# Hybrid decoder trunk on one core: six pairs of the first up projection's wide group as seven-product sets, with side work that pauses

## The chip, the cores and the metric

The kernel runs on one core of one Trainium2 chip. The metric is the device time of one execution in microseconds (us); the figure of a version is the median of its runs. The engines are TensorE (PE; its weight loads are shown as PEld), VectorE (DVE), ScalarE (ACT), GpSimd (POOL) and SyncE (SP). Each has a queue of its own and works through it in order. They wait for one another by semaphores. DMA transfers are issued here from SP (weights) and from POOL (side work).

## The reference

Two layers of a decoder over 256 positions of width 2048. What matters here, cut:

```python
for layer in range(DEPTH):
    if layer % 2 == 0:
        mix = even_mixer(h, ...)   # SSD heads and MoBA attention heads, then one output projection
    else:
        mix = odd_mixer(h, ...)    # NSA attention heads and retention heads, then one output projection
    h = layer_norm(DEEPNORM_ALPHA * h + mix, ...)
    ffn = conv_ffn(h, ffn_w_up[layer], ffn_conv_w[layer], ffn_conv_b[layer], ffn_w_down[layer])
    h = layer_norm(DEEPNORM_ALPHA * h + ffn, ...)

def conv_ffn(x, w_up, conv_w, conv_b, w_down):
    a, u = jnp.split(x @ w_up, 2, axis=-1)
    a = causal_depthwise_conv(a, conv_w, conv_b)
    return (jax.nn.silu(a) * u) @ w_down
```

`w_up` has 2 x 5632 columns. All is float32.

## The kernel before

**Products in three matmuls.** A float32 product is made of reduced-precision parts: each weight slab comes by DMA into one of six buffers `wraw` (L185), ACT copies its rounded value `whi` (L210), DVE subtracts to get the rest `wlo` (L218), and PE adds three products, high by high, high by low and low by high. `Weights.get` keeps the splits three slabs ahead of PE (`AHEAD = 3`); there are four buffers each for `whi` and `wlo`.

**Groups.** A projection runs as a list of jobs. `group_b` (matmuls on L427) makes 256 columns of the output over all 16 k tiles of x; a slab holds four k tiles. `group_m` (L539 to L541) makes 1024 columns and takes the k tiles in pairs. A pair is a two by two block product: k tiles by the two halves of 256 positions, against the two halves of 1024 columns. Planned "P" (plain) it is 8 products of three matmuls. Planned "N" or "R" it is a set of 7 products after the Strassen-Winograd scheme, which needs sums of weight blocks and sums of activation blocks. For "N" the weight sums are made on the spot by four DVE additions (`add_up`, L229), into the tile `other` in an up projection. For "R" they were made earlier: the slab "T" is loaded from a DRAM scratch. An "N" pair loads two slabs of 512 KB, an "R" pair three of 512 KB and one of 256 KB, a "P" pair two of 512 KB. The activation sums come from `sum_up` (L499 on; L509, L513 and the splits on L337 and L338).

**The up projections.** `ffn(layer)` runs `group_b` for most of the 44 column blocks; block 7 of layer 0, and blocks 4, 8 and 12 of layer 1, are "wide": one `group_m` with `inner` makes four groups' columns. In both layers its eight pairs are planned "NPNPNPNP".

**Work between the matmuls.** `Fill` is a list of steps; after every second k tile of a `group_b` one step is popped from `self.fill` and one from `self.aux`. A number in the list is that many empty steps. In `ffn`, `self.fill` carries the side work: `cycles` makes the weight sums for later sets ("R"), one set at a time in the tile `sums` (or two in turn with `second`). A set is two loads issued by POOL (L240), the additions on DVE (L246), two stores issued by POOL (L250). Its period in steps is the third figure of `CYCLES` per layer (13 and 14; 10 for the six sets of layer 0 that use two tiles). `self.aux` carries the residual's multiplications (L873, L877) and the `sum_up` calls. Inside a `group_m` with `inner` only `self.aux` is popped. The tile framework orders instructions on an engine by readiness, except those that are pinned with `keep_in_program_order`; loads, additions and stores of the side work are pinned.

**The first attention.** In `even`, twelve `group_b` jobs (four gates z, then queries and keys of eight heads) run with the SSD scan and the attention heads as steps in `self.fill` at rate 0.80; nothing is in `self.aux` there. The scan makes decay products on DVE (L1340) that PE uses (L1355); POOL adds squares (L1368) and takes a power (L1378) that PE uses in `scale` (L1387). An attention head ends in `mix` (L1161), which multiplies the probabilities by V.

Of the kernel before, what the change touches and what calls it, by code (L numbers as in the profile page):

```python
# [34 lines left out]
        ("od_in", 0): "NPNPNPNP", **{(f"up{i}", p): "NPNPNPNP" for i in range(2) for p in range(3)}}  # L35
WIDE_UP = ((7,), (4, 8, 12))
FIRST = (22, 30)
CYCLES = ((6, 10, 13), (0, 0, 14))
SEVEN = {"down0": (1, 3, 5, 7, 9, 11, 13, 15, 16, 17, 14), "down1": (1, 3, 5, 7, 9, 11, 13, 14, 15),
         "ev_out": (0, 1, 2, 3), "od_out": (0, 1, 2, 3),  # L40
         "od_in": (0, 1, 2, 3), "up0": (0, 1, 2, 3), "up1": (0, 1, 2, 3)}
# [81 lines left out]
class Weights:  # L123
# [107 lines left out]
    def make(self, key, dram, s):  # L231
# [12 lines left out]
        def add():  # L244
            for o, x, y in ((b11, b11, b12), (b12, b12, b22), (b22, b11, b22), (b21, b22, b21)):
                self.tc.keep_in_program_order(nc.vector.tensor_tensor(o, x, y, op=OP.add))  # L246
# [5 lines left out]
        return load, add, store  # L252
# [69 lines left out]
class Trunk:  # L322
# [160 lines left out]
    def cycles(self, keys, bufs, period):  # L483

        fill, made = self.fill, [self.w.make(k, self.dram, bufs[i % len(bufs)]) for i, k in enumerate(keys)]
        n, wait = len(bufs), min(5, period - 4)
        fill.add(made[0][0])
        if n == 1:
            fill.add(period - 4 - wait)
        else:  # L490
            fill.add(3, made[1][0], 6)
        for i, (_, add, store) in enumerate(made):
            fill.add(add, 1, store)
            if i + n < len(made):
                fill.add(wait, made[i + n][0])
            if i + 1 < len(made):
                fill.add(period - 4 - wait)

    def sum_up(self, act, pair, u):  # L499
# [10 lines left out]
        a11, a21, a12, a22 = v[:, 0, :128], v[:, 0, 128:], v[:, 1, :128], v[:, 1, 128:]  # L510
        s1, s2, s4, s3 = (u[:, 128 * i:128 * i + 128] for i in range(4, 8))
        for o, p, q in ((s1, a21, a22), (s2, a11, s1), (s4, a12, s2), (s3, a21, a11)):
            nc.vector.tensor_tensor(o, p, q, op=OP.subtract)  # L513
        self.split(hi, lo, u[:, 512:896])
        self.split(*last, s3)

    def group_m(self, act, src, p, c, gap=1, fresh=None, inner=None):
# [73 lines left out]
        it = iter(index)  # L591
        for j, plan in pairs:
            k = 2 * j
            if plan != "P":
# [3 lines left out]
                add("P2", at(k + 1, 0), wt, 0)  # L598
                add("P3", s4, wt, 512)
                wt = w.get(next(it))  # L600
                add("P4", at(k + 1, 1), wt, 0)
# [11 lines left out]
            else:  # L613
                for kk in range(k, k + 2):
                    wt = w.get(next(it))
                    for n, t, o in (("P2", 0, 0), ("P4", 1, 0), ("P3", 0, 512), ("B8", 1, 512)):
                        add(n, at(kk, t), wt, o, whole and kk == 2 * pairs[-1][0] + 1)
# [468 lines left out]
    def attn_steps(self, P, y, ct, h, branches, gate=None, cmp=None):  # L1086
# [61 lines left out]
        def mix():  # L1148
            o = self.ps()
            for t in range(2):  # L1150
                mms = []
                for b, (_, _, v) in enumerate(branches):
                    pt = st["pt"][b]
                    if t == 0:
                        mms.append((v(0), pt[:, 0:128]))
                    else:
                        mms += [(v(0), pt[:, 128:256]), (v(1), pt[:, 256:384])]
                if cmp:
                    mms.append((cmp[0], cmp[1][:, t * 128:(t + 1) * 128]))
                for i, (a, b) in enumerate(mms):  # L1160
                    nc.tensor.matmul(o[:, t * 128:(t + 1) * 128], a, b, start=(i == 0), stop=(i == len(mms) - 1))  # L1161
            self.split(y[:, ct, :256], y[:, ct, 256:], o[:, :256])
# [4 lines left out]
    def even(self):  # L1167
        nc, x = self.nc, self.x
        with ExitStack() as ctx:
# [63 lines left out]
            with self.tc.tile_pool(name="even2", bufs=1) as P2:  # L1233
# [5 lines left out]
                self.fill.rate = 0.80  # L1239
                for i in range(4):  # L1240
# [392 lines left out]
    def ffn(self, layer):  # L1633
        nc, x = self.nc, self.x
        with ExitStack() as ctx:
# [11 lines left out]
            if wide:  # L1647
# [66 lines left out]
            for i, e in enumerate(evacs[3:], 3):  # L1714
# [11 lines left out]
                elif j not in wide and j - 1 not in wide:  # L1726
# [142 lines left out]
```

## Time and profile before

| | |
|---|---|
| runs | 2248.83 us median of 3 (2248.74 to 2249.03) |
| profiled execution | span 2246.8 us from the first to the last instruction; its own time outside the span isn't recorded beside it |
| first attention phase (twelve `group_b`) | 133 to 297 us |
| `up0`, with its wide group | 372 to 820 us; wide group about 528 to 568 us |
| `up1`, first of its three wide groups | about 1611 to 1651 us |
| mean granted TensorE clock | 0.999 |

The phases' bounds are read from the chain of work in order of time and from the timeline. A row of a timeline reads: start, duration, engine, line, operation, tiles, shapes, count, and in brackets the idle time of the engine before it with what ended it. A row of the waits reads: who waited for whom, total us, times, longest. Durations of neighbouring matmuls overlap; the pace of PE is the distance of their starts.

### The profile page before, as it was taken

How to read it: one execution, taken by the hardware profiler on the slowest of the kernel's cores; microseconds unless marked ns; L12 is line 12 of the kernel's file. 1: busy time of each engine (PE TensorE's matmuls, PEld its weight loads, DVE VectorE, ACT ScalarE, POOL GpSimd, SP SyncE). 2: the span in 40 equal slices, each digit the busy share in tenths (PEclk: the TensorE clock that was granted, in tenths of full speed). 3: DMA queues.
4: the chain of work that ended last, by engine and by line, in shares of the span. 5: the costliest groups of instructions: out<-in, count | busy, mean ns of one | idle time of the engine just before them, and what ended most of it. 6: DMA issues, size and time to landing. Idle time of an engine off the chain costs nothing.

```text
span 2246.8 us, 32995 instructions
## 1 busy us (share of the span) xinstructions
PE 2235.3 (99%) x12125; PEld 1920.9 (85%) x12125; DVE 1831.3 (82%) x2795; ACT 1254.0 (56%) x1718; POOL 126.4 (6%) x219
## 2 busy tenths in 40 slices
PE   9999999999999999999999999999999999999998
PEld 9888888888888888888898888888888888888887
DVE  5788688988877778887977777889988887779887
ACT  5555555655555556656645564457555565557563
POOL 0101000110011100000000000000100001100000
PEclk9999999999999999999999999999999999999999
DMA  9854456897788886888668534467876768888884
GB/s 312 292 175 161 158 194 189 274 376 264 238 302 302 296 284 213 292 286 274 211 208 287 188 114 154 152 209 235 290 227 228 255 217 297 300 273 276 276 280 169
DMA packets 158780, 546.33 MB, mean 243 GB/s; under 512 B 17827, under 2 KB 19283, under 8 KB 158483
## 3 DMA queue, kind: packets, MB, share of 16 engines
q1 hardware_dynamic: 132937, 451.41, 60.1%
q0 software_dynamic: 25536, 92.55, 11.8%
q8 instruction: 95, 1.56, 0.3%
q14 instruction: 68, 0.56, 0.1%
q10 hardware_dynamic: 144, 0.26, 0.0%
HBM read 502.19 MB, written 41.96 MB: 242 GB/s over the span
## 4 chain that ended last, share of the span: by engine, by line
PE 96%; DVE 2%; issue 1%; ACT 0%; POOL 0%; DMA 0%; SPq 0%; ACTq 0%; POOLq 0%; DVEq 0%
PE acc L427 51%; PE ps L540 7%; PE ps L541 7%; PE ps L539 7%; PE acc L627 3%; PE acc L629 3%; PE acc L628 3%; PE acc L540 3%; PE acc L541 3%; PE acc L539 3%; PE ps L628 1%; PE ps L627 1%; PE ps L629 1%; PE ps L1161 1%; PE ps L427 1%
## 5 line engine op out<-in xcount | busy, mean ns | idle before, releaser
L210 ACT ACTIVATE whi<-wraw 128x1024 fp32r<-128x1024 f32 (+4 forms) x882 | 875.1, 1002 | 549.6 <-PE acc L427 219.0
L218 DVE TENSOR_TENSOR wlo<-wraw,whi 128x1024 fp32r<-128x1024 f32 (+4 forms) x882 | 1007.5, 1153 | 209.6 <-ACT whi L210 197.6
L427 PE MATMUL acc<-x,whi 128*128 128x512 f32 x3296 | 1032.2, 398 | 0.0
L427 PEld LDWEIGHTS acc<-x,wlo 128*128 128x128 f32 x3296 | 604.0, 188 | 136.5 <-DVE wlo L218 0.3
L427 PE MATMUL acc<-x,wlo 128*128 128x256 f32 x3296 | 633.8, 279 | 0.0
L427 PEld LDWEIGHTS acc<-x,whi 128*128 128x128 f32 x3296 | 510.0, 189 | 9.7 <-issue 1.1
L689 ACT ACTIVATE tmp<-acc 128x512 f32<-128x512 f32 x104 | 62.2, 598 | 167.8 <-PE acc L427 167.7
L246 DVE TENSOR_TENSOR sums<-sums 128x512 f32<-128x512 f32 x140 | 96.2, 687 | 10.5 <-DMA sums<-in_down 9.4
L540 PE MATMUL ps<-wlo,g 128*128 128x512 f32 x260 | 101.3, 390 | 0.0
L541 PE MATMUL ps<-whi,g 128*128 128x512 f32 x260 | 101.2, 389 | 0.0
L539 PE MATMUL ps<-whi,g 128*128 128x512 f32 x260 | 101.2, 389 | 0.0
L539 PE MATMUL ps<-whi,x 128*128 128x512 f32 x244 | 94.0, 390 | 2.7 <-ACT whi L210 2.7
L540 PE MATMUL ps<-wlo,x 128*128 128x512 f32 x244 | 95.5, 391 | 0.1
L541 PE MATMUL ps<-whi,x 128*128 128x512 f32 x244 | 95.0, 389 | 0.0
L627 PE MATMUL acc<-whi,x 128*128 128x344 f32 (+3 forms) x224 | 74.9, 336 | 0.7 <-ACT whi L210 0.7
L628 PE MATMUL acc<-wlo,x 128*128 128x344 f32 (+3 forms) x224 | 74.5, 333 | 0.3 <-DVE wlo L218 0.3
L629 PE MATMUL acc<-whi,x 128*128 128x344 f32 (+3 forms) x224 | 74.3, 332 | 0.0
L1681 DVE SCALAR_TENSOR_TENSOR c<-fpad,prm,c 128x256 f32<-128x256 f32 x176 | 74.2, 479 | 0.0
L210 ACT ACTIVATE whi<-other 128x1024 fp32r<-128x1024 f32 x32 | 33.7, 1055 | 57.7 <-DVE other L229 56.9
L250 POOL DMA_DIRECT2D sumdown<-sums x62 | 33.3, 537 | 570.9 <-DVE sums L246 570.8
L540 PEld LDWEIGHTS ps<-wlo,g 128*128 128x128 f32 x260 | 48.8, 188 | 10.5 <-DVE wlo L218 0.4
L539 PEld LDWEIGHTS ps<-whi,g 128*128 128x128 f32 x260 | 48.8, 188 | 10.3
(458 smaller groups left out, 3141.6 us busy)
## 6 DMA issues: line engine op xcount, KB each, us to landing
wraw<-in_up SPq DMA_DIRECT2D x328, 512.0 KB, 4.8
wraw<-in_down SPq DMA_DIRECT2D x142, 512.0 KB, 4.8
wraw<-in_od_in SPq DMA_DIRECT2D x96, 512.0 KB, 4.2
wraw<-in_ev_in SPq DMA_DIRECT2D x72, 512.0 KB, 4.1
wraw<-sumdown SPq DMA_DIRECT2D x68, 512.0 KB, 4.5
sums<-in_down POOLq DMA_DIRECT2D x62, 512.0 KB, 6.8
sumdown<-sums POOLq DMA_DIRECT2D x62, 512.0 KB, 5.4
wraw<-in_ev_out SPq DMA_DIRECT2D x30, 512.0 KB, 3.9
```

Source lines behind the costliest of these rows:

```text
L210: a = nc.scalar.activation(hi[:, :n], raw[:, :n], AF.Copy)
L218: b = nc.vector.tensor_tensor(lo[:, :n], raw[:, :n], hi[:, :n].bitcast(F32), op=OP.subtract)
L246: self.tc.keep_in_program_order(nc.vector.tensor_tensor(o, x, y, op=OP.add))
L427: nc.tensor.matmul(acc, wt, mv, start=(k == 0 and i < len(unit)), stop=(k == nk - 1 and i >= len(unit)))
L539: nc.tensor.matmul(o, xh, wh, start=n not in used, stop=False)
L540: nc.tensor.matmul(o, xh, wl, start=False, stop=False)
L541: nc.tensor.matmul(o, xl, wh, start=False, stop=stop)
L627: nc.tensor.matmul(o, xh, wh, start=start, stop=False)
L628: nc.tensor.matmul(o, xh, wl, start=False, stop=False)
L629: nc.tensor.matmul(o, xl, wh, start=False, stop=stop)
L689: nc.scalar.activation(t, a[:, :, 256:], AF.Copy, scale=sign)
L1681: nc.vector.scalar_tensor_tensor(c[:, i, :], pad[:, i, t:t + 256], w[:, t:t + 1], c[:, i, :], op0=OP.mult, op1=OP.add)
```

## The change

- The plan of the wide group of `up0` goes from "NPNPNPNP" to "RRRPRRRP": six sets whose weight sums are loaded, two plain pairs. Six activation sums are made for it, in six tiles `part` instead of four.
- The six sets' weight sums are made in the first attention phase, by `cycles` with period 14 in `self.aux`.
- In `cycles` the additions of a set are separate steps, and they are three operations instead of four (one over 1024 columns makes two sums). The waits between steps are laid out anew; the period of layer 1 goes from 14 to 12.
- Eight empty steps are put at the head of `self.fill` before the last `group_b` ahead of each wide group.
- `sum_up` makes two of its four subtractions in one.
- `mix` multiplies by V(0) once over 256 positions instead of twice over 128.
- Stop flags in `group_m` follow the new order of the pairs.

```diff
-        ("od_in", 0): "NPNPNPNP", **{(f"up{i}", p): "NPNPNPNP" for i in range(2) for p in range(3)}}
+        ("od_in", 0): "NPNPNPNP", ("up0", 0): "RRRPRRRP", **{("up1", p): "NPNPNPNP" for p in range(3)}}
-CYCLES = ((6, 10, 13), (0, 0, 14))
+CYCLES = ((6, 10, 13), (0, 0, 12))
-         "od_in": (0, 1, 2, 3), "up0": (0, 1, 2, 3), "up1": (0, 1, 2, 3)}
+         "od_in": (0, 1, 2, 3), "up0": (0, 1, 2, 3, 4, 5), "up1": (0, 1, 2, 3)}
...
-        def add():
-            for o, x, y in ((b11, b11, b12), (b12, b12, b22), (b22, b11, b22), (b21, b22, b21)):
-                self.tc.keep_in_program_order(nc.vector.tensor_tensor(o, x, y, op=OP.add))
+        first, both = s[:, 0:1024].rearrange("p (i c) -> p i c", i=2), s.rearrange("p (i c) -> p i c", i=4)[:, 1:4:2, :]
+
+        def add(o, x, y):
+            return lambda: self.tc.keep_in_program_order(nc.vector.tensor_tensor(o, x, y, op=OP.add))
+
+        adds = [add(*a) for a in ((first, first, both), (b22, b11, b22), (b21, b22, b21))]
...
-    def cycles(self, keys, bufs, period):
+    def cycles(self, keys, bufs, period, fill=None):
...
-        n, wait = len(bufs), min(5, period - 4)
+        n = len(bufs)
         fill.add(made[0][0])
-        if n == 1:
-            fill.add(period - 4 - wait)
-        else:
+        if n == 2:
             fill.add(3, made[1][0], 6)
-        for i, (_, add, store) in enumerate(made):
-            fill.add(add, 1, store)
+        for i, (_, adds, store) in enumerate(made):
+            if n == 1:
+                fill.add(5)
+            fill.add(*adds, store)
+            if i + 1 < len(made):
+                fill.add(period - (10 if n == 1 else 6))
             if i + n < len(made):
-                fill.add(wait, made[i + n][0])
-            if i + 1 < len(made):
-                fill.add(period - 4 - wait)
+                fill.add(made[i + n][0])
+            if n == 2:
+                fill.add(1)
...
-        s1, s2, s4, s3 = (u[:, 128 * i:128 * i + 128] for i in range(4, 8))
-        for o, p, q in ((s1, a21, a22), (s2, a11, s1), (s4, a12, s2), (s3, a21, a11)):
+        s3, s1, s2, s4 = (u[:, 128 * i:128 * i + 128] for i in range(4, 8))
+        ends = u[:, 0:512].rearrange("p (i t) -> p i t", i=4)[:, 0:4:3, :]
+        for o, p, q in ((u[:, 512:768].rearrange("p (i t) -> p i t", i=2), a21[:, None, :].to_broadcast([128, 2, 128]), ends),
+                        (s2, a11, s1), (s4, a12, s2)):
             nc.vector.tensor_tensor(o, p, q, op=OP.subtract)
...
-                        add(n, at(kk, t), wt, o, whole and kk == 2 * pairs[-1][0] + 1)
+                        add(n, at(kk, t), wt, o, kk > k and (end or whole and n == "B8" and j == plain))
...
-            for t in range(2):
-                mms = []
-                for b, (_, _, v) in enumerate(branches):
-                    pt = st["pt"][b]
-                    if t == 0:
-                        mms.append((v(0), pt[:, 0:128]))
-                    else:
-                        mms += [(v(0), pt[:, 128:256]), (v(1), pt[:, 256:384])]
-                if cmp:
-                    mms.append((cmp[0], cmp[1][:, t * 128:(t + 1) * 128]))
-                for i, (a, b) in enumerate(mms):
-                    nc.tensor.matmul(o[:, t * 128:(t + 1) * 128], a, b, start=(i == 0), stop=(i == len(mms) - 1))
+            mms = [(v(0), pt[:, 0:256], 0) for (_, _, v), pt in zip(branches, st["pt"])]
+            mms[1:1] = [(v(1), pt[:, 256:384], 128) for (_, _, v), pt in zip(branches, st["pt"])]
+            if cmp:
+                mms[1:1] = [(cmp[0], cmp[1], 0)]
+            for i, (a, b, c) in enumerate(mms):
+                nc.tensor.matmul(o[:, c:256], a, b, start=(i == 0), stop=(i == len(mms) - 1))
...
                 self.fill.rate = 0.80
+                self.cycles(self.keys("up0"), [self.w.sums], 14, self.aux)
...
-                self.slots = [E.tile([128, 1024], F32R, name=f"part{i}") for i in range(4)]
+                self.slots = [E.tile([128, 1024], F32R, name=f"part{i}") for i in range(len(SEVEN[f"up{layer}"]))]
...
+                for step in sums[4:]:
+                    self.aux.add(3, step)
...
                 elif j not in wide and j - 1 not in wide:
+                    if j + 1 in wide and i % 2:
+                        self.fill.q[:0] = [lambda: None] * 8
                     self.group_b(x, [e])
```

More of the change, by code (lines that the diff above doesn't have):

```diff
@@ L250, in store @@
                 self.tc.keep_in_program_order(nc.gpsimd.dma_start(self.made[key][i], s[:, 1024 * i:1024 * i + 1024]))
-        return load, add, store
+        return load, adds, store
     def pump(self, n, pin=False):
@@ L481, in keys @@
         return [k for s in src for k in self.w.made if k[0] == s]
-    def cycles(self, keys, bufs, period):
-        fill, made = self.fill, [self.w.make(k, self.dram, bufs[i % len(bufs)]) for i, k in enumerate(keys)]
-        n, wait = len(bufs), min(5, period - 4)
+    def cycles(self, keys, bufs, period, fill=None):
+        fill, made = fill or self.fill, [self.w.make(k, self.dram, bufs[i % len(bufs)]) for i, k in enumerate(keys)]
+        n = len(bufs)
         fill.add(made[0][0])
-        if n == 1:
-            fill.add(period - 4 - wait)
-        else:
+        if n == 2:
             fill.add(3, made[1][0], 6)
-        for i, (_, add, store) in enumerate(made):
-            fill.add(add, 1, store)
+        for i, (_, adds, store) in enumerate(made):
[4 more added lines that the diff above has]
+                fill.add(period - (10 if n == 1 else 6))
             if i + n < len(made):
-                fill.add(wait, made[i + n][0])
-            if i + 1 < len(made):
-                fill.add(period - 4 - wait)
+                fill.add(made[i + n][0])
+            if n == 2:
+                fill.add(1)
     def sum_up(self, act, pair, u):
@@ L509, in sum_up @@
         nc.vector.tensor_tensor(v, act[:, k:k + 2, :256].bitcast(F32), act[:, k:k + 2, 256:].bitcast(F32), op=OP.add)
-        a11, a21, a12, a22 = v[:, 0, :128], v[:, 0, 128:], v[:, 1, :128], v[:, 1, 128:]
-        s1, s2, s4, s3 = (u[:, 128 * i:128 * i + 128] for i in range(4, 8))
-        for o, p, q in ((s1, a21, a22), (s2, a11, s1), (s4, a12, s2), (s3, a21, a11)):
+        a11, a21, a12 = v[:, 0, :128], v[:, 0, 128:], v[:, 1, :128]
+        s3, s1, s2, s4 = (u[:, 128 * i:128 * i + 128] for i in range(4, 8))
+        ends = u[:, 0:512].rearrange("p (i t) -> p i t", i=4)[:, 0:4:3, :]
+        for o, p, q in ((u[:, 512:768].rearrange("p (i t) -> p i t", i=2), a21[:, None, :].to_broadcast([128, 2, 128]), ends),
+                        (s2, a11, s1), (s4, a12, s2)):
             nc.vector.tensor_tensor(o, p, q, op=OP.subtract)
-        self.split(hi, lo, u[:, 512:896])
+        self.split(hi, lo, u[:, 640:1024])
         self.split(*last, s3)
@@ L591, in group_m @@
         it = iter(index)
+        plain = [j for j, plan in pairs if plan == "P"][-1]
         for j, plan in pairs:
             k = 2 * j
+            end = whole and j == pairs[-1][0]
             if plan != "P":
@@ L597, in group_m @@
                 wt = w.get(next(it))
-                add("P2", at(k + 1, 0), wt, 0)
-                add("P3", s4, wt, 512)
+                add("P2", at(k + 1, 0), wt, 0, end)
+                add("P3", s4, wt, 512, end)
                 wt = w.get(next(it))
-                add("P4", at(k + 1, 1), wt, 0)
+                add("P4", at(k + 1, 1), wt, 0, end)
                 fill.pop()
```

## The prediction

> **What bounds the kernel now.** I read the page first: the span, the engines' busy shares, and the chain that ended last.
>
> ```profile
> span 2246.8 us, 32995 instructions
> PE 2235.3 (99%) x12125; PEld 1920.9 (85%) x12125; DVE 1831.3 (82%) x2795; ACT 1254.0 (56%) x1718; POOL 126.4 (6%) x219
> ...
> PE 96%; DVE 2%; issue 1%; ACT 0%; POOL 0%; DMA 0%; SPq 0%; ACTq 0%; POOLq 0%; DVEq 0%
> ```
>
> TensorE (PE) is busy nearly all of the span and the chain is 96% PE. So only two things shorten the time: PE instructions that go, and PE waits that go. The next view is the list of PE's waits.
>
> ```profile
> PE ps L539 <- ACT whi L210: 2.7, 2, 1.5
> PE ps L1760 <- DVE ones L1757: 1.1, 1, 1.1
> ```
>
> The longest wait by far is at L539, inside `group_m`, twice in the whole run. The timeline places it: the second pair of the wide group of `up0` (539 us) and the second pair of the first wide group of `up1` (1622 us).
>
> ```profile
> 537.57 0.69 DVE L229 TENSOR_TENSOR other<-other,wraw 128x512 f32<-128x512 f32 x1
> 538.17 0.69 DVE L229 TENSOR_TENSOR other<-wraw 128x512 f32<-128x512 f32 x1
> 538.77 0.69 DVE L229 TENSOR_TENSOR other<-other,wraw 128x512 f32<-128x512 f32 x1
> 539.08 0.39 PE L539 MATMUL ps<-whi,part 128*128 128x512 f32 x1
> 539.58 1.06 ACT L210 ACTIVATE whi<-other 128x1024 fp32r<-128x1024 f32 x1 [6.08 <-DVE other L229]
> 540.69 0.50 PE L539 MATMUL ps<-whi,x 128*128 128x512 f32 x1 [1.22 <-ACT whi L210]
> 541.02 0.40 PE L540 MATMUL ps<-wlo,x 128*128 128x512 f32 x1
> ...
> 1615.02 0.69 DVE L246 TENSOR_TENSOR sums<-sums 128x512 f32<-128x512 f32 x1
> 1619.70 0.69 DVE L246 TENSOR_TENSOR sums<-sums 128x512 f32<-128x512 f32 x1
> 1621.50 0.69 DVE L229 TENSOR_TENSOR other<-other,wraw 128x512 f32<-128x512 f32 x1
> 1621.81 0.39 PE L539 MATMUL ps<-whi,part 128*128 128x512 f32 x1
> 1622.59 1.06 ACT L210 ACTIVATE whi<-other 128x1024 fp32r<-128x1024 f32 x1 [6.42 <-DVE other L229]
> 1623.69 0.50 PE L539 MATMUL ps<-whi,x 128*128 128x512 f32 x1 [1.50 <-ACT whi L210]
> ```
>
> Both times VectorE (DVE) is behind: a plan "N" pair makes its weight sums in place (L229, four additions), between them run four additions of the side work (L246), and ScalarE (ACT) can split the sum only when L229 is through.
>
> **The pace of PE.** Durations of matmuls overlap, so I take start to start, from the same wide group:
>
> ```profile
> 529.99 0.39 PE L540 MATMUL ps<-wlo,x 128*128 128x512 f32 x1
> ...
> 531.58 0.39 PE L541 MATMUL acc<-whi,x 128*128 128x512 f32 x1
> ```
>
> These two rows are seven matmuls apart: 1.59 / 7 = 0.227 us each. The 0.39 in the rows is a duration and would overstate every saving.
>
> The Trainium skill ("TensorE: Matmul & The Clock Gate", part 1) gives a warm matmul its columns over 2.4 GHz plus about 2.5 ns, 215.7 ns for 512 columns; the six matmuls below would then be 1.29 us instead of 1.36, and the measured 227 ns decides.
>
> **Part 1, six pairs as sets.** A plain pair ("P") is 8 products of 3 matmuls, a set ("N" or "R") 7 of 3. Four of eight pairs were sets already ("NPNPNPNP"), six will be ("RRRPRRRP"). Two pairs lose 3 matmuls each: 6 x 0.227 = **1.36 us** off PE.
>
> **Part 2, the wait at 539 us.** The "R" pairs read their sums from DRAM, so all L229 additions leave this group, and the pause of 8 steps keeps the L246 additions out of its start. The wait is 540.69 - 539.08 - 0.227 = 1.38, and the matmul after it starts 0.33 later instead of 0.227, 0.10 more: **1.48 us** goes. What is late next? DVE needs three splits of 1024 columns and one of 512 per set, bounded by the rows in part 4 with 3 x 1.22 + 0.69 = 4.35 us, against 21 x 0.227 = 4.77 us of PE: DVE keeps up. The weights are the tighter side. A set now loads 3.5 slabs of 524,288 bytes, 1.835 MB in 4.77 us, which is 385 GB/s; three sets and a plain pair are 6.55 MB in 19.74 us, 332 GB/s.
>
> ```profile
> 480.00:500.00 20.00, 20.00 (x116) 17.49 (x115) 18.14 (x25) 11.03 (x15) 4.30 (x8) 1.00 1.00 383
> 900.00:1040.00 140.00, 140.00 (x618) 115.50 (x617) 116.64 (x144) 83.73 (x95) 0.00 (x0) 1.00 0.82 284
> ```
>
> In these windows (columns: busy PE, PEld, DVE, ACT, POOL, clock, DMA share, GB/s) the DMA engines moved 383 GB/s at share 1.00, and 284 at 0.82, that is some 346 when full. Three sets at 346 GB/s take 5.5 MB / 346 = 15.9 us against 14.3 of PE; the 1.6 us short are covered by the six weight buffers (3.1 MB), which the slower groups ahead fill. I cost it at nothing; uncovered it is 1.6 us a run of sets, 3.2 in all.
>
> The Trainium skill ("DMA: Bandwidth & Descriptors", Where 436 GB/s comes from) holds that reads from HBM are bound near 358 GB/s per core, which speaks against three sets in a row; it would make the shortfall 15.4 - 14.3 = 1.1 us a run; the 383 above contains writes, so no row here refutes it.
>
> **Part 3, the wait at 1622 us.** The plan of `up1` stays "NPNPNPNP"; only the pause helps. The four L246 additions between 1615.02 and 1619.70 were issued by the last group ahead, which now issues none. They hold DVE for 4 x 0.60 = 2.4 us (0.60 is the step between the neighbouring rows at 537.57, 538.17 and 538.77). The wait is 1623.69 - 1621.81 - 0.227 = 1.65, with the same 0.10 after it **1.75 us**. 2.4 is more than 1.65, so it goes whole unless other work takes the place. The shorter period (14 to 12 steps) makes up for the pauses: a step is two of the k tiles of a `group_b`.
>
> ```profile
> 589.65 273.60 PE acc L427 x1568
> sums<-in_down POOLq DMA_DIRECT2D x62, 512.0 KB, 6.8
> sumdown<-sums POOLq DMA_DIRECT2D x62, 512.0 KB, 5.4
> ```
>
> 1568 matmuls, 8 to a step, are 196 steps in 273.6 us: 1.40 us a step. A set of sums now has 9 steps from its store to the next additions, 12.6 us, for a store of 5.4 and a load of 6.8, 12.2 together. That is close: an addition may wait at the head of DVE's queue, with the weight splits behind it. These run up to three slabs ahead of PE (`AHEAD`; a slab is four k tiles, 2.8 us), so I cost it at nothing, bounded by that whole chain's overrun of some 1 us for each of 15 sets if the lead is gone. The count of steps fits: about 240 of some 247 pops in `up1`, 283 of 297 in `up0`, so no rest is flushed at the end.
>
> **Part 4, six sums in the first attention.** They go into `aux` ahead of the gate projections: 80 steps, and 12 groups of 8 pops give 96, so they end inside this phase. Each set adds, on POOL's queue, two loads and two stores of 512 KB, and on DVE one addition of 1024 columns and two of 512.
>
> ```profile
> L218 DVE TENSOR_TENSOR wlo<-wraw,whi 128x1024 fp32r<-128x1024 f32 x743 | 900.6, 1222 | 179.3 <-ACT whi L210 168.9
> L246 DVE TENSOR_TENSOR sums<-sums 128x512 f32<-128x512 f32 x140 | 96.2, 687 | 10.5 <-DMA sums<-in_down 9.4
> ```
>
> A set costs 1.22 + 2 x 0.69 = 2.6 us of DVE, six 15.6 us; DMA moves 6 x 4 x 0.524 = 12.6 MB more.
>
> ```profile
> 133.00:297.00 164.00, 164.00 (x1015) 142.79 (x1014) 122.04 (x237) 85.42 (x143) 10.28 (x8) 1.00 0.49 160
> 160.00:180.00 20.00, 20.00 (x133) 17.43 (x132) 19.37 (x37) 12.01 (x19) 2.09 (x1) 1.00 0.47 159
> 200.00:220.00 20.00, 20.00 (x143) 17.09 (x142) 18.45 (x35) 10.26 (x18) 2.90 (x2) 1.00 0.50 158
> ```
>
> Over the phase DVE has 42 of 164 us free and DMA half its time, so the mean has room: 12.6 MB in 164 us is 77 GB/s on top of 160. But in two stretches, the chunked scan of the SSD heads, DVE is 97% and 92% busy, and PE waits there for products of DVE:
>
> ```profile
> 215.16 0.55 DVE L1340 TENSOR_TENSOR pt<-pt,cbm 128x384 f32<-128x384 f32 x1
> 216.66 0.80 PE ps L1355 x10
> ```
>
> The last decay product ends at 215.7 and PE uses it at 216.6: 0.9 us to spare. With 14 steps to a set and some 1.6 us to a step here, the fourth set's additions (steps 49 to 51 from 133 us) fall near 210 us. All 2.6 us ahead of that product would stall PE 1.7 us; none of it, nothing. Spread over three steps, with about one of the three ahead of it, I take **+0.4 us**; the range keeps 0 to 1.7, and that once for each of the two dense stretches at worst. On POOL's queue a load waits for the store before it to land, with the additions of `xs` and the power of the RMS norm queued behind it, which PE reads two or more steps later. The load comes five steps (8 us) after the store, landing takes 5.4, so it is hidden; late by 2 us it would cost PE at most that, at the two RMS steps. SP's queue is passed by nothing: the sets' slabs stand where the "N" slabs stood, and their sums were stored some 270 us earlier. The changed stop flags of `group_m` add no instruction.
>
> Two more calls of `sum_up` for the activations (six DVE operations of at most 0.69 us, two ACT splits) lie in `up0`, in the stretch where the window 480 to 500 us shows DVE at 18.1 of 20 and PE without a gap; hidden by the same three slabs, at most 4 us each if not. The merged subtractions and additions save DVE a fixed part each and PE nothing.
>
> **Part 5, fewer PV records.** A float32 matmul appears as two records. An even head goes from 3 matmuls to 2, an odd head from 8 to 5; the columns that stream stay the same (384 and 1024). 8 x 2 x 1 + 8 x 2 x 3 = 64 pairs of 128-column records become one of 256.
>
> ```profile
> 1285.04 1.78 PE ps L1161 x16
> L1161 PE MATMUL ps<-pt,V 128*128 128x128 f32 x48 | 6.5, 274 | 0.0
> L1105 PE MATMUL ps<-k,q 128*128 128x256 f32 x16 | 4.8, 380 | 0.0
> ```
>
> A 128-column record takes 1.78 / 16 = 111 ns, and one of 256 columns lasts 380 - 274 = 106 ns longer, so 217. A merge saves 2 x 111 - 217 = 5 ns, 64 of them **0.3 us**. The bounds are nothing and the whole second start, which no row here puts above some 10 ns: 0.6.
>
> **The sum**, against the profiled execution: 1.36 + 1.48 + 1.75 + 0.3 - 0.4 = 4.5 us off a span of 2246.8. The three runs' median is 2248.83, 2.0 above the span; what lies around the span is left as it is, so 2248.83 - 4.5 = **2244.4 us** (rounded from 2244.34).
>
> **The rivals.** (a) *A wait stays or moves.* Side work that is paused comes back elsewhere; the residual's multiplications and the paused additions can crowd the same start of the `up1` wide group, since DVE was at its limit there. Against it: 2.4 us freed against a wait of 1.65. If one of the two stays, the time is 2245.9 or 2246.1; if both, 2247.6. (b) *The loads bind*: three sets in a row outrun DMA. 332 GB/s on average against some 346 leaves little. Price up to 3.2: 2247.6. (c) *The other side*: DVE in the attention phase becomes the bound. Each addition waits at the head of DVE's queue for its load (the step count doesn't wait for a landing), and the decay products and splits stand behind it. The profile's loads land in 6.8 us; from load to addition there are 6 steps, some 9.6 us here: the wait decides once a load takes longer than that. Then every set costs PE what the 0.9 us to spare doesn't cover, 2.6 - 0.9 = 1.7, six times 10.2, in place of the 0.4 above: 2248.83 - 4.9 + 10.2 = 2254.1. For it speaks the 97% stretch; against it 6.8 and a DMA share of 0.49. (d) *The change doesn't do what it says*: the plan is read, but the additions are pushed past their pauses because the order on DVE follows readiness; then 1.66 for parts 1 and 5 is all that comes, 2247.2. It shares its price with (a). (e) *More goes*: the side work split into steps also removes small waits that the list of waits doesn't show, 1 us more: 2243.3.
>
> **How the numbers follow.** The forecast (2243.6 to 2245.2) has 0.46; (a) and (d) together 0.24; (b) 0.11; (c) 0.07, in half of which only some of the six sets are hit; (e) 0.12. The range of 8 in 10 takes in the forecast, (a), (d), (b) and the nearer part of (e) and leaves out (c) and (e)'s far part: 2243.0 to 2247.8. A change of 0.2%, 4.5 us, is about what a measurement of this kernel can tell from none. Faster by more is below 2244.33, which cuts the forecast's own range in the middle: half of 0.46 and all of (e), 0.23 + 0.12 = 0.35. Slower by more, above 2253.3, is the full (c), 0.04. The rest, 0.61, is within 0.2%.
>
> **What would show it.** Part 1: 174 matmuls instead of 180 in the wide group of `up0`, L229 gone there. Parts 2 and 3: no PE wait at L539 in the list of waits. Part 4: no new PE wait at L1355, L1387 or L427 between 133 and 297 us, and the six sets' stores landed there. Part 5: 64 records fewer in the group of `mix`, those of 256 columns some 217 ns start to start. The forecast is wrong if a wait on `wlo` or `whi` appears in the wide group of `up0` (loads), if the wait at 1622 us stays, or if the attention phase is longer by over 1 us.

## The result, and the profile after

The changed kernel takes **2267.85 us** (median of 4 runs, 2266.07 to 2268.68) against 2248.93 for the kernel before on the same chip (2248.74 to 2251.11): a ratio of 1.0082, 95% interval 1.0069 to 1.0096. It is slower by 18.9 us, where 4.5 us less was forecast. The profiled execution's span grew from 2246.8 to 2264.3 us.

First the page of the changed kernel: span, busy shares, the engines' shares of the chain that ended last, and the group of the side work's additions (L247, which was L246 before).

```profile
span 2264.3 us, 32879 instructions
PE 2241.0 (99%) x12055; PEld 1918.9 (85%) x12055; DVE 1834.6 (81%) x2735; ACT 1257.4 (56%) x1726; POOL 137.9 (6%) x243
...
PE 85%; DMA 6%; issue 5%; DVE 4%; POOL 0%; ACT 0%; SPq 0%; DVEq 0%; POOLq 0%; ACTq 0%
...
L247 DVE TENSOR_TENSOR sums<-sums 128x512 f32<-128x512 f32 (+1 forms) x123 | 106.1, 863 | 70.5 <-DMA sums<-in_down 67.2
```

TensorE (PE) has 70 records fewer and still takes longer. The chain was 96% PE; now DMA and VectorE (DVE) hold 10% of it. The additions' last column says where: DVE stood idle 67.2 us at the head of its queue until a load of the side work landed (9.4 before). The list of PE's waits:

```profile
PE acc L430 <- DVE wlo L218: 8.4, 5, 2.5
PE ps L1298 <- DVE neg L1293: 2.1, 1, 2.1
PE acc L547 <- DVE wlo L218: 1.6, 3, 1.3
PE ps L1378 <- POOL xs L1372: 1.5, 1, 1.5
```

The two waits at L539 of before are gone, as meant. Four others head the list now. (Lines have moved: the matmuls of `group_b` are on L430 now, those of `group_m` on L546 to L548, the side work's stores on L253, the residual on L878 to L886.)

**Where the time went.** I take each matmul of `group_b` with the high part of a weight (the same number in the same order in every version), and subtract its start in before's trace from its start in the other. This gives how late the kernel is at that matmul. The columns are the matmul's time in before, in us; "end" is the end of the span. Only the difference of two columns says what a stretch costs. Each row is one execution, the profiled one (for e2 and e7 the longest of their runs), so rows of versions whose code is the same in a stretch can still differ there.

```
time in before            53   223   514   580  1605  1672  1915  2010   end
after                    0.5   6.9   6.2   3.3   2.7   4.1   4.6  16.2  17.4
e1 period 14             0.3   4.1   3.5   0.9   0.6  -0.5  -0.5  -0.5  19.7
e2 additions in one step 0.7   8.2   7.6   4.8   4.2  11.2  11.2  11.2  12.0
e3 no pause              0.5   8.1   8.3   7.7   7.2   9.6   9.5  18.7  18.6
e4 up0 as before         0.1  -0.1  -0.8  -2.1  -2.7  -0.7  -0.2  11.8  11.8
e5 PV records alone      0.7   0.7   0.5   0.5   0.1   0.0   0.0   0.0   0.3
e6 period 14, no pause   0.1   7.8   7.1   8.5   7.9   8.1   8.1   8.1   7.9
e7 sums 12 steps later   0.0   1.0   0.3  -2.6  -3.2  -1.1  -0.4  12.9  14.2
e8 PV, pause in up0      0.5   0.5   0.3  -1.0  -1.4  -1.2  -1.2  -1.2  -1.3
e9 e7, period 14, 1 pause 0.1  1.1   0.4  -2.7  -3.0  -3.4  -3.3  -3.3  -3.6
e10 e7, up1 as before    0.1   1.1   0.4  -2.3  -2.9  -1.6  -1.6  -1.6  -1.8
e11 rows on SP           0.1   5.9   5.2   3.6   3.2   1.5   2.1  14.5  15.5
```

In the changed kernel the first attention phase (53 to 223) costs 6.4 us, the wide group of `up0` (514 to 580) gives 2.9, the first wide group of `up1` (1605 to 1672) costs 1.4 where it was to give 1.75, and the last stretch of `up1` (1915 to 2010) costs 11.5 with no wide group in it.

**The last stretch.** The timeline of DVE in the changed kernel, the first additions of four sets in turn after the last wide group, which ends at 1834 (the bracket is DVE's idle time before it), and what follows one of them:

```profile
1868.70 1.22 DVE L247 TENSOR_TENSOR sums<-sums 128x1024 f32<-128x1024 f32 x1 [2.86 <-DMA sums<-in_down]
1888.13 1.22 DVE L247 TENSOR_TENSOR sums<-sums 128x1024 f32<-128x1024 f32 x1 [3.88 <-DMA sums<-in_down]
1905.99 1.23 DVE L247 TENSOR_TENSOR sums<-sums 128x1024 f32<-128x1024 f32 x1 [5.84 <-DMA sums<-in_down]
1925.74 1.23 DVE L247 TENSOR_TENSOR sums<-sums 128x1024 f32<-128x1024 f32 x1 [6.40 <-DMA sums<-in_down]
1926.88 1.22 DVE L218 TENSOR_TENSOR wlo<-wraw,whi 128x1024 fp32r<-128x1024 f32 x1
1928.02 0.68 DVE L247 TENSOR_TENSOR sums<-sums 128x512 f32<-128x512 f32 x1
1928.62 1.22 DVE L218 TENSOR_TENSOR wlo<-wraw,whi 128x1024 fp32r<-128x1024 f32 x1
1929.76 0.68 DVE L247 TENSOR_TENSOR sums<-sums 128x512 f32<-128x512 f32 x1
```

The idle time grows turn by turn, 2.86, 3.88, 5.84, 6.40, and in the four turns after these it is 5.3 to 6.5. At 6.4 the splits behind the addition (L218) come too late and PE stops, for the first time at 1928:

```profile
1924.60 1.09 PE L430 MATMUL acc<-x,whi 128*128 128x512 f32 x4
1928.16 0.51 PE L430 MATMUL acc<-x,wlo 128*128 128x256 f32 x2 [2.46 <-DVE wlo L218]
```

The chain of waits in this window shows the loop that DVE waits for (start, length, what):

```profile
1925.74 0.07 DVE sums L247
...
1929.76 0.69 DVE sums L247
1930.45 0.28 issue
1930.73 5.44 DMA sumdown<-sums
1936.17 0.28 issue
1936.46 7.25 DMA sums<-in_down
...
1943.80 0.09 DVE sums L247
```

This is a closed ring: three additions with two splits between them (4.71 us), the store (5.44), the load, which on POOL's queue stands behind the landing of that store (7.25), and the next additions; with the issue gaps 1943.80 - 1925.74 = 18.06 us. The next turns start at 1962.41 and 1980.59: 18.3 us a turn on average. The plan gives a set 12 steps of 1.40 us, 16.8. So each turn is 1.5 us late. The weight splits' lead covers the first turns. After that the ring, not PE, sets the pace. Of the 11.5 us, 8.4 are the five waits at L430, and a fall of the clock (last section) makes some 1.7 more.

### The profile page after: what moved, and what is told of

The parts are those of the page before. It is cut to its first block, busy times and chain, and to the rows that moved or that the text cites. A ratio compares the mean times of both kernels' runs of the same rounds, so it can differ in the third digit from the quotient of the medians.

```text
span 2264.3 us, 32879 instructions
## 1 busy us (share of the span) xinstructions
PE 2241.0 (99%) x12055; PEld 1918.9 (85%) x12055; DVE 1834.6 (81%) x2735; ACT 1257.4 (56%) x1726; POOL 137.9 (6%) x243
## 4 chain that ended last, share of the span: by engine, by line
PE 85%; DMA 6%; issue 5%; DVE 4%; POOL 0%; ACT 0%; SPq 0%; DVEq 0%; POOLq 0%; ACTq 0%
PE acc L430 41%; PE ps L547 7%; PE ps L546 7%; PE ps L548 7%; PE acc L547 3%; PE acc L548 3%; PE acc L546 3%; PE acc L636 3%; PE acc L637 3%; PE acc L638 3%; DMA sums<-in_down 3%; DMA sumdown<-sums 2%; DVE wlo L218 1%; PE ps L636 1%; PE ps L637 1%
## 5 line engine op out<-in xcount | busy, mean ns | idle before, releaser
L210 ACT ACTIVATE whi<-wraw 128x1024 fp32r<-128x1024 f32 (+4 forms) x894 | 886.1, 1001 | 538.1 <-PE acc L430 199.1
L218 DVE TENSOR_TENSOR wlo<-wraw,whi 128x1024 fp32r<-128x1024 f32 (+4 forms) x894 | 1018.8, 1151 | 184.4 <-ACT whi L210 172.1
L430 PE MATMUL acc<-x,whi 128*128 128x512 f32 x3296 | 1035.4, 399 | 0.0
L430 PEld LDWEIGHTS acc<-x,wlo 128*128 128x128 f32 x3296 | 604.9, 188 | 147.5 <-DVE wlo L218 11.3
L430 PE MATMUL acc<-x,wlo 128*128 128x256 f32 x3296 | 636.0, 280 | 8.4 <-DVE wlo L218 8.4
L430 PEld LDWEIGHTS acc<-x,whi 128*128 128x128 f32 x3296 | 512.0, 189 | 10.1 <-issue 1.3
L247 DVE TENSOR_TENSOR sums<-sums 128x512 f32<-128x512 f32 (+1 forms) x123 | 106.1, 863 | 70.5 <-DMA sums<-in_down 67.2
L546 PE MATMUL ps<-whi,g 128*128 128x512 f32 x260 | 101.3, 390 | 0.1
L548 PE MATMUL ps<-whi,g 128*128 128x512 f32 x260 | 101.2, 389 | 0.0
L548 PE MATMUL ps<-whi,x 128*128 128x512 f32 x232 | 90.5, 390 | 0.0
L546 PE MATMUL ps<-whi,x 128*128 128x512 f32 x232 | 90.0, 390 | 0.0
L253 POOL DMA_DIRECT2D sumdown<-sums x62 | 33.3, 538 | 596.9 <-DVE sums L247 596.6
L1684 ACT ACTIVATE c<-fpad,prm 128x256 f32<-128x256 f32 x88 | 47.9, 592 | 35.7 <-DVE fpad L701 35.5
L546 PEld LDWEIGHTS ps<-whi,g 128*128 128x128 f32 x260 | 48.8, 188 | 10.7 <-DVE r L716 0.5
```

The costliest lines, as they stand in the source:

```text
L210: a = nc.scalar.activation(hi[:, :n], raw[:, :n], AF.Copy)
L218: b = nc.vector.tensor_tensor(lo[:, :n], raw[:, :n], hi[:, :n].bitcast(F32), op=OP.subtract)
L247: return lambda: self.tc.keep_in_program_order(nc.vector.tensor_tensor(o, x, y, op=OP.add))
L430: nc.tensor.matmul(acc, wt, mv, start=(k == 0 and i < len(unit)), stop=(k == nk - 1 and i >= len(unit)))
L546: nc.tensor.matmul(o, xh, wh, start=n not in used, stop=False)
L548: nc.tensor.matmul(o, xl, wh, start=False, stop=stop)
```

## The experiments

Each edit is against the changed kernel unless it says otherwise. The first four are about the end of `up1`.

**e1, period 14**

```diff
-CYCLES = ((6, 10, 13), (0, 0, 12))
+CYCLES = ((6, 10, 13), (0, 0, 14))
```

> The changed kernel with one figure back: the period of layer 1's side work is 14 steps again instead of 12. Theory A (closed chain): a set of sums is a ring of two loads, three additions, two stores, and a load that waits for the store to land; in the changed kernel's trace one turn takes 18.3 us at the end of the second up projection (first store at 1927.26, next first store at 1945.59), more than 12 steps of 1.4 us (16.8 us). DVE then stands 6.5 us at the head of its queue in every turn and TensorE runs out of weights. 14 steps are 19.5 us, more than the turn: the stretch from the third wide group to the down projection loses most of the 11.6 us it grew by, time near 2257 us. Rival B (more DVE work or its order through the pauses) and rival C (the merged addition that needs both loads): the period doesn't matter, within 3 us of 2267.9.

Measured 2271.24 us, ratio 1.0096 (1.0081 to 1.0111). The loss from 1915 to 2010 is gone (-0.5 before, -0.5 after), and so are the waits at L430. But 20 us are lost behind it, between 2010 and the end. PE's longest wait and the windows there (us; busy PE, PEld, DVE, ACT, POOL; clock; DMA share; GB/s):

```profile
PE ps L546 <- ACT x L340: 12.9, 1, 12.9
```

```profile
2010.00:2035.00 25.00, 22.64 (x98) 17.86 (x96) 16.91 (x29) 9.96 (x12) 2.69 (x5) 1.00 0.77 290
2035.00:2056.00 21.00, 7.14 (x16) 4.92 (x17) 13.56 (x16) 7.75 (x9) 0.54 (x1) 0.51 0.49 165
```

With 14 steps a set and the pauses, the side work doesn't fit into `up1`: 21 steps were left over, by a count of the program's steps, and they are flushed before `down1` begins, stores, loads and additions one after the other. So the shorter period was needed for the pauses, and it was the shorter period that, with the additions drawn apart (e2), made the ring longer than the plan.

**e2, the additions of a set in one step**

```diff
-            fill.add(*adds, store)
+            fill.add(lambda adds=adds: [f() for f in adds], store)
             if i + 1 < len(made):
-                fill.add(period - (10 if n == 1 else 6))
+                fill.add(period - (8 if n == 1 else 4))
```

> The changed kernel with the three additions of a set in one step instead of three; period 12 kept, the two steps go between store and next load. Theory A: splitting lengthened the ring by up to two steps (2.8 us); without it a turn is some 15.5 to 16.5 us, under 16.8, and most of the 11.6 us goes: near 2257 to 2260 us. Rival C (the merged addition): still merged, stays within 3 us of 2267.9. Rival D (a burst of additions holds up weight splits, the reason to split them): slower than 2267.9.

Measured 2256.87 us, 1.0038 (1.0025 to 1.0051). The period stays 12, the merged addition stays, the pauses stay, and the loss from 1915 to 2010 is gone. The chain of waits of this version from 1900 to 1985 us is one piece:

```profile
1899.97 85.13 PE acc L430 x488
```

So neither the period alone nor the merged addition makes the loss. The two steps by which the additions were drawn apart are part of the ring. Without them the turns from 1909.43 to 2011.87 us take 17.1 on average, 0.3 more than 12 steps, and DVE still stands idle for a load, 0.5 to 5.3 us a turn; but the splits' lead lasts to the end. Seven us are lost elsewhere, from 1605 to 1672, in the first wide group of `up1` (see e11 and the last section).

**e3, no pauses**

```diff
-                    if j + 1 in wide and i % 2:
-                        self.fill.q[:0] = [lambda: None] * 8
```

> The changed kernel without the eight empty steps ahead of each wide group. Theory A: the turns stay too long, so the stretch at the end of the second up projection keeps its loss within 3 us; only the starts of the wide groups move, by 1 to 2 us each. Rival B: the pauses push the side work together, and without them the loss at the end shrinks by over 6 us.

Measured 2267.25 us, 1.0074 (1.0057 to 1.0091). The last stretch still costs 18.7 - 9.5 = 9.2 us: the pauses aren't its cause. In the wide group of `up0` the gain falls from 2.9 to 0.6 us.

**e6, period 14 and no pauses** (both edits above)

> The changed kernel with period 14 and without the pauses, so that all steps fit ahead of the down projection (in E1 21 steps were left over and ran in one go there). Theory A (the ring of 18.3 us against the period): no loss at the end of the second up projection, as in E1, and none at the start of the down projection: the end stands within 2 us of where the third wide group stands against before. The first phase keeps its 4 to 6 us, the first up projection gains about 1.4 to 3 us. Near 2252 us. Rival: the pauses were what kept the end of E1 free; without them some of the 11 us comes back, over 2258 us.

Measured 2256.02 us, 1.0031 (1.0019 to 1.0043). No loss from 1672 to 2010, no flush at the end. Without the pause the wide group of `up0` is 1.4 us slower than before's, though it has six sets; PE waits there 1.5 us for a split, and the clock falls for a time behind that (see the last section). In e3, whose code is the same up to there, that wait is 1.1 us, the clock doesn't fall, and 0.6 us is gained.

The next two are about the first attention phase.

**e4, `up0` as before**: plan "NPNPNPNP", four activation sums, no `cycles` in the attention.

```diff
-        ("od_in", 0): "NPNPNPNP", ("up0", 0): "RRRPRRRP", **{("up1", p): "NPNPNPNP" for p in range(3)}}
+        ("od_in", 0): "NPNPNPNP", ("up0", 0): "NPNPNPNP", **{("up1", p): "NPNPNPNP" for p in range(3)}}
...
-         "od_in": (0, 1, 2, 3), "up0": (0, 1, 2, 3, 4, 5), "up1": (0, 1, 2, 3)}
+         "od_in": (0, 1, 2, 3), "up0": (0, 1, 2, 3), "up1": (0, 1, 2, 3)}
...
-                self.cycles(self.keys("up0"), [self.w.sums], 14, self.aux)
```

> The changed kernel with the first wide group planned as before (four sets made on the spot, four plain pairs) and no sums made in the first attention. Theory: the phase up to the first layer norm loses the 6.4 us it grew by (371.2 against 364.8 us for its transposes), and the first up projection gives back its gain of 2.95 us, or half of that if the pause alone takes away the wait at 539 us: near 2264 to 2265 us. Rival: the growth of the first phase comes from the V product in fewer records or from the order of the schedule, not from the sums: the phase keeps over 4 us of it and the time is near 2270 us.

Measured 2261.42 us, 1.0056 (1.0041 to 1.0071). The loss from 53 to 223 us is gone (-0.2), so it comes from the sums. Its size isn't fixed: e1, e3, e6 and e11 have the changed kernel's code in this phase and lose 3.8, 7.6, 7.7 and 5.8 us there, where the changed kernel lost 6.4. The wide group keeps 1.3 us of its gain, by the pause alone.

**e7, the same sums, begun 12 steps later**

```diff
+                self.aux.add(12)
                 self.cycles(self.keys("up0"), [self.w.sums], 14, self.aux)
```

> The changed kernel with the six sums of the first attention begun 12 steps later, past the softplus of the SSD heads. Theory H (the first phase loses where an addition falls into a serial row of small DVE operations or ahead of a decay product that TensorE waits for): the wait of 2.1 us at the cumulation of the decays (142 us) goes, and the others move; the phase loses 2 to 5 instead of 6.4 us. Rival I (DVE or DMA as a whole is too full in this phase): the phase loses the same 6 us in other places.

Measured 2260.01 us, 1.0048 (1.0031 to 1.0065). The same six sets, with the same loads, additions and stores in the same phase, now cost 1.0 us from 53 to 223 instead of 6.4; against e4, which has none, 1.2 instead of 6.6; e9 and e10, with the same later sums, lose 1.0 each. So it is not the amount of work but what it meets. In the changed kernel it meets two serial chains. One is the softplus at the phase's start (timeline of the changed kernel; in before's trace L1282 to L1289, the same chain, ended at 138.68 + 0.19, and PE's matmul that reads the result started at 142.21):

```profile
127.96 1.20 POOL L240 DMA_DIRECT2D sums<-in_up  x2 [33.71 <-DVE nb L1075]
...
135.36 1.23 DVE L247 TENSOR_TENSOR sums<-sums 128x1024 f32<-128x1024 f32 x1 [2.06 <-DMA sums<-in_up]
...
140.34 0.68 DVE L247 TENSOR_TENSOR sums<-sums 128x512 f32<-128x512 f32 x1
140.94 0.18 DVE L1286 TENSOR_TENSOR sp_p<-sp_p,sp_s 128x32 f32<-128x32 f32 x1
141.04 1.22 DVE L218 TENSOR_TENSOR wlo<-wraw,whi 128x1024 fp32r<-128x1024 f32 x1
142.18 0.22 DVE L1287 TENSOR_SCALAR sp_p<-sp_p 128x32 f32<-128x32 f32 x1
142.26 1.22 DVE L218 TENSOR_TENSOR wlo<-wraw,whi 128x1024 fp32r<-128x1024 f32 x1
143.40 0.18 DVE L1286 TENSOR_TENSOR sp_p<-sp_p,sp_s 128x32 f32<-128x32 f32 x1
...
144.29 0.19 DVE L1293 SCALAR_TENSOR_TENSOR neg<-dt,sp_a 128x32 f32<-128x32 f32 x1
```

Small operations of 0.2 us, each dependent on the one before it, find additions and splits of 0.7 to 1.2 us between them. These use up the 3.3 us that the chain had to spare in before; it ends 5.6 us later here. On top of that the first set's addition stands 2.06 us at the head of DVE's queue for its load, with the rest of the softplus behind it: POOL issued that load only at 127.96, after a wait for a copy out of the tile `sums` (L1075), and DVE came to the addition at 133.30. PE waits 2.13 us for the last operation (L1298). The six versions that begin the sums here show the two together: DVE's wait for this load is 1.05, 1.35, 1.56, 1.72, 1.80 and 2.06 us (e1, e11, e2, e6, e3, after), and PE's wait at L1298 is some 0.08 longer each time. In e7 the first addition comes at 150.81, behind the softplus and without a wait. The other chain is the RMS norm: the third set's additions (181.7 to 187.1) push back what POOL and PE need at 194.4 (L1378, 1.5 us). The products ahead of it ran at 184.60 in before (L1362) and at 188.59 here (L1366). In e7 neither wait is in the list.

**e11, the residual's rows from another queue.** POOL issues the rows `room` behind the side work's loads. Here SP issues them in layer 1.

```diff
-                self.pin(nc.gpsimd.dma_start(tiles[i][which], self.row(idx, which, 512 * i, 512)))
+                self.pin((rows or nc.gpsimd).dma_start(tiles[i][which], self.row(idx, which, 512 * i, 512)))
...
-                self.residual(2 * layer, [[room[:, 0:512], room[:, 512:1024]]] * 4, self.aux, sums)
+                self.residual(2 * layer, [[room[:, 0:512], room[:, 512:1024]]] * 4, self.aux, sums, nc.sync if layer else None)
```

> The changed kernel with the rows for layer 1's residual (tile room) loaded from SyncE's queue instead of GpSimd's. Theory K (the loss at the first wide group of layer 1 comes from these rows standing on GpSimd's queue behind loads of the side work that wait for a store to land; VectorE then waits at the residual's multiplication, 1.98 us in the changed kernel's trace): the stretch from 1605 to 1672 us, 1.44 us longer than before, is up to 1.7 us shorter than before or the same; the end of the second up projection keeps its loss: near 2265 us. Rival (the loss is VectorE's amount of work there): the stretch keeps its 1.4 us.

Measured 2264.02 us, 1.007 (1.0056 to 1.0084). From 1605 to 1672 it gains 1.7 us where the changed kernel loses 1.4. What was in the way there, in the timeline of the changed kernel:

```profile
1606.04 0.53 POOL L240 DMA_DIRECT2D sums<-in_down  x1 [4.09 <-DMA sumdown<-sums]
1606.57 1.07 POOL L878 DMA_DIRECT2D room<-in_lnrow  x2
...
1613.50 0.69 DVE L882 SCALAR_TENSOR_TENSOR r<-r,room 128x512 f32<-128x512 f32 x1 [1.98 <-DMA room<-in_lnrow]
1614.11 1.22 DVE L218 TENSOR_TENSOR wlo<-other,whi 128x1024 fp32r<-128x1024 f32 x1
```

and in that of e2, where the same wait is longer and PE waits 3.9 us behind it:

```profile
1619.00 0.69 DVE L882 SCALAR_TENSOR_TENSOR r<-r,room 128x512 f32<-128x512 f32 x1 [3.74 <-DMA room<-in_lnrow]
1619.61 1.22 DVE L218 TENSOR_TENSOR wlo<-other,whi 128x1024 fp32r<-128x1024 f32 x1
```

POOL waits 4.09 us for the landing of a store of the side work before it can issue the load, the rows stand behind it, the residual's multiplication (L882) stands at the head of DVE's queue for the rows, and the split that PE needs stands behind that. In before's trace the rows were issued at 1599.58 and 1601.32. In e1, where the period of 14 puts the rows ahead of the loads on POOL's queue (1600.70 and 1602.71), the same stretch gains 1.1 us. The late loss stays in e11 (2.1 to 14.5), so the rows aren't its cause.

Two small versions, against the kernel before. **e5, the merged `mix` alone** (the last hunk of the change's diff):

> The kernel before with only the V product merged (64 pairs of records become one). In E4 the first attention was 0.77 us and the second about 0.6 us shorter than before. Theory F (each record that goes saves some 20 ns, not the 5 ns of the prediction): 1.2 to 1.4 us in the two attentions, 2247.6 us. Rival G (5 ns, the rest is the changed order of the schedule): 0.3 us, 2248.7 us.

Measured 2248.28 us (10 runs) beside 2248.72, ratio 0.9998 (0.9989 to 1.0007): no difference that the runs can tell. Between the traces' matmuls it gains 0.1 us in the first attention and 0.5 in the second.

**e8, the merged `mix`, and the pause in layer 0 alone**

```diff
+                    if layer == 0 and j + 1 in wide and i % 2:
+                        self.fill.q[:0] = [lambda: None] * 8
```

> The kernel before with two parts of the change: the merged V product, and the eight empty steps ahead of the wide group of the first up projection alone. The wait at 539 us goes by the pause alone (in E4 this stretch gained 1.3 us): 2249.0 - 1.3 (V product, or 0.3) - 1.4 = 2246.3 to 2247.3 us.

Measured 2247.28 us (10 runs), 0.9994 (0.9985 to 1.0003). From 514 to 580 its trace gains 1.3 us, as e4's does; the runs' times alone leave "no difference" open.

**e9 and e10: two versions that keep what was shown to help.** Both begin the sums 12 steps later (e7) and take period 14. In e9 the pause and the six empty steps behind a wide group stand, in `up1`, only at the first of its three wide groups, so that all steps fit (`up0` has one wide group and keeps them):

```diff
-                    self.fill.q[:0] = [lambda: None] * 6
+                    self.fill.q[:0] = [lambda: None] * (6 if j == wide[0] else 0)
...
-                    if j + 1 in wide and i % 2:
+                    if j + 1 == wide[0] and i % 2:
```

> The changed kernel with the six sums begun 12 steps later (E7), period 14 in layer 1 (E6), and the eight empty steps ahead of the first wide group of layer 1 alone, without the empty steps after the others, so that all steps fit. Theories A and H together: the first phase loses 0 to 0.5 us, the first up projection gains 2.9, the second attention's V product 0.5, the start of the first wide group of layer 1 gains 1.1 as in E1, and nothing is lost at the end of the second up projection: 2248.9 - 4.2 = 2244.7 us. If the gain of E1 at that wide group hung on where its additions happened to fall, up to 2 us are lost there: 2247.8 us.

Measured **2245.73 us** (11 runs, 2244.94 to 2247.69), ratio to before 0.9986 (0.9978 to 0.9995). It beats both kernels. Its list of PE's waits and its window over the last stretch:

```profile
PE ps L1769 <- DVE ones L1766: 1.1, 1, 1.1
PE acc L547 <- DVE wlo L218: 0.8, 1, 0.8
```

```profile
1915.00:2010.00 95.00, 95.00 (x542) 82.80 (x541) 69.71 (x83) 48.97 (x61) 9.65 (x18) 1.00 0.83 281
```

In the changed kernel PE was busy 88.27 of these 95 us. e10 leaves layer 1's side work laid out as before, without the pause:

> As E9, but layer 1's side work laid out as before the change (all additions in one step, period 14, no pauses). Theories A and H: the gains up to the second up projection stay (3.2 us in E7), layer 1 is as before, its wait at 1622 us included: 2248.9 - 3.2 = 2245.7 us. Rival (the splitting of the additions was needed): layer 1 loses over 2 us.

Measured 2246.47 us (11 runs), 0.9991 (0.9982 to 1.0). From 1605 to 1672 it loses 1.3 us where e9 gains 0.4. Layer 1's additions are in one step there, and the pause is missing; which of the two it is, no run here tells apart.

## Why the prediction was wrong

**Part 1 and Part 2 (six sets, the wait at 539 us) held.** Predicted 1.36 + 1.48 = 2.84 us off the wide group of `up0`; measured 2.95 in the changed kernel and 3.06 in e9. The pause alone gives 1.3 of it (e4, e8). Rival (b), that the loads bind there, fell: no wait on a load in that group, and the first set's 21 matmuls take 4.8 us there (534.63 to 539.43), as forecast. But Part 2 named the leaving of the additions L229 and the pause together, and with the sets and no pause the group is 1.4 us slower than before in e6 and 0.6 faster in e3, one execution each of the same code: the pause carries that part.

**Part 3, the wait at 1622 us: right only where the rows don't stand behind a store.** Predicted 1.75 us gone; measured 1.4 lost, and 1.68 gained in e11 once the rows leave POOL's queue (1.1 in e1, where they stand ahead of the loads). The step that failed is "2.4 is more than 1.65, so it goes whole unless other work takes the place". Rival (a) named the residual's multiplications as what may crowd the place. It had the instruction right; the price was off, since it counted their DVE time and not that they wait for rows behind a store on POOL's queue.

**Part 3, the shorter period: this step failed most.** The prediction counted "9 steps from its store to the next additions, 12.6 us" against "a store of 5.4 and a load of 6.8, 12.2 together", saw that it was close, and went on: "These run up to three slabs ahead of PE ..., so I cost it at nothing". Two things were wrong. It compared one leg of the ring with its steps and left out the other: the additions in their three steps, with splits between them, take 4.7 us from the first's start to the last's end, where three steps are 4.2, so that a whole turn is 18.3 us against 16.8. The leg that it did compare was too long as well: in the turn shown, 5.44 and 7.25 with 0.66 of issue gaps are 13.35 us against 12.6, so of this turn's 1.3 us too much 0.75 come from there and 0.5 from the additions. And it set a lead, which can be used up once, against a lateness that comes again each turn. The trace shows it going: 2.86, 3.88, 5.84, 6.40. The prediction even worked out the bound, "some 1 us for each of 15 sets if the lead is gone", 15 us in all; the 11.5 from 1915 to 2010 lie within it. It then left that bound out of the sum and of the range. e1 and e6 (longer period) and e2 (shorter ring) each take the loss away; e3 and e11 don't.

**Part 4: the mechanism fell.** Predicted +0.4, with 0 to 1.7 for each of two stretches; measured 6.4, and 3.8 to 7.7 in other executions of this code. The prediction looked at the decay products at L1355, where the trace shows no wait in the list. The price was paid at the softplus and at the RMS norm, and raised by the clock: of the 6.4, 2.4 had come by the matmul at 144 us in before's time, the RMS norm's gap is 1.5, and the halved clock behind it (below) some 1.7. The prediction argued from busy shares of 20 us; a chain of short dependent operations has no busy share to speak of and is delayed by every long operation on its engine. Rival (c) had the side and, for one set of six, the mechanism: an addition at the head of DVE's queue that waits for its load. Its 9.6 us from load to addition were 5.3 for the first set, whose load POOL could issue only at 127.96. What stood behind was the softplus and not a decay product, and it cost PE 2.1 us, not 10.2; with more time for that load e7 loses 1.0 in all.

**Part 5 was right, its size small by half.** Predicted 0.3 with the upper bound 0.6; e5 shows 0.1 and 0.5 us in the two attentions, 0.6, some 9 ns for each of 64 merges. The runs alone can't tell it from nothing.

**The sum.** All the gains were found where they were forecast, 2.95 + 0.6, and with e11's 1.68 they are 5.2 us against a forecast of 4.9. What was wrong is the price of added side work: nothing for the period, 0.4 for the sums, because another thing was to cover it.

## What to carry to other kernels

A side job that stores, loads and computes in one buffer is a ring: add up all its legs, the compute with what is queued between its parts too, and compare a whole turn with its period; a lead of buffers covers a single delay, not one that comes every turn. Work added to an engine with free time is to be placed by the chains of short dependent operations that run there, and by when its first load can be issued, not by the busy share; moving it 12 steps took the loss from 6.4 us to 1.0 in these traces. And a queue that waits for a store to land delays everything issued behind it, so rows that are needed soon belong on another.

## What the runs showed of the hardware

The granted clock of TensorE fell to half after gaps of PE as short as 1.5 us, in some executions and not in others. In e4 it was 0.50 from 1616 to 1618 us after two gaps, of 0.56 and 1.30 us (1612.57 and 1614.34). After the RMS norm's gap of 1.48 us in the changed kernel, and after the gap of 2.46 at 1928, the windows (last three columns: clock, DMA share, GB/s) read:

```profile
195.00:199.00 4.00, 4.00 (x16) 3.49 (x16) 2.05 (x4) 0.00 (x0) 1.94 (x2) 0.57 0.89 322
...
1929.00:1933.00 4.00, 4.00 (x16) 3.46 (x15) 3.97 (x6) 0.07 (x1) 1.07 (x2) 0.57 1.00 297
```

and in e1, after the same gap of 1.48 us at the same place:

```profile
195.00:199.00 4.00, 4.00 (x26) 3.55 (x25) 2.13 (x5) 1.48 (x2) 0.75 (x1) 1.00 0.94 303
```

16 matmuls in 4 us against 26. The gap at the RMS norm is 1.5 us in six versions (after, e1, e2, e3, e6, e11); in five of them the clock fell behind it, in e1 it didn't. The two drops above lasted 3.4 us each by the starts of the matmuls, and cost some 1.7 us more than the gap itself, an estimate from 3.4 us at half the clock; by the lateness of the matmuls the first cost 1.6 us against e1. In e2, after the gap of 3.9 us in the first wide group of `up1`, the drop lasted 10.2 us, three times as long:

```profile
1620.00:1630.00 10.00, 8.46 (x19) 6.19 (x20) 9.96 (x14) 2.52 (x3) 0.00 (x0) 0.50 0.29 92
```

Before's gaps of 1.22 and 1.50 us, and the changed kernel's of 2.13 at the softplus, were followed by none. The Trainium skill ("TensorE: Matmul & The Clock Gate", What's actually happening) puts the drop after at least one idle window of about 3.4 us; here gaps of less than half of that were followed by one, while the lengths 3.4 and 10.2 agree with one and three such windows. What decides between a gap with a drop and one without isn't settled by these runs. For an estimate, a PE gap of 1.5 us or more can be priced too low by its own length.
